# A hybrid decoder layer on one core: three quarters of the output projection moved among the small products of the last head pair

## The chip, the core and the metric

The kernel runs on one of the eight cores of a Trainium2 chip. TensorE (PE) multiplies, and its weight loads are listed apart (PEld); VectorE (DVE), ScalarE (ACT) and GpSimd (POOL) do the elementwise work; SyncE (SP) issues nearly all DMAs. SBUF holds tiles of 128 partitions, and PSUM has eight banks of 128 x 512 float32 values for the results of PE. The metric is the device time of one launch in microseconds, as the median of several runs.

## What is computed

The reference is one decoder layer over 512 tokens and 16 meta tokens, width 1024, in float32:

```
h      = layer_norm([meta, x], ln0)                      # 528 x 1024
proj   = h @ w_in                                        # q, k, v, r/k/v/w/a/g of RWKV-7, two gates
att    = sliding-window attention with sinks (16 heads of 64)
rw     = RWKV-7 time mixing: a recurrence over time, 16 heads of 64
merged = sigmoid(gate_att) * att + sigmoid(gate_rwkv) * rw
h      = layer_norm(ALPHA * h + merged @ w_out, ln1)     # w_out: 1024 x 1024
ff     = square(relu(h @ w_ff1)) @ w_ff2                 # 1024 -> 4096 -> 1024
out    = layer_norm(ALPHA * h + ff, ln2)                 # the 512 tokens
```

The matrix product in the middle, `merged @ w_out`, is the output projection that the change moves.

## The kernel before

**Products.** Each float32 operand of a large product is split into a high and a low part (`split`, L253, two ACT casts of 128 x 512 and two DVE subtractions), and three matmuls stand for one product: high x high, high x low, low x high (`three`, L332; `project_out`, L1390). The normalized input lies in `hhi` and `hlo`, eight tiles k of 128 channels by 528 tokens (L279). A dense unit (`dense`, L348) is one column block of 128 of `w_in` and has eight steps, one for each k.

**Stages.** Heads go in pairs j = 0 to 7, and the loop of L1319 goes through stages s = -1 to 8. In stage s, PE runs the small products of three things: the solve and the state chain of pair s-1 (`solve`, L1277: blocks, start, inverse, fold, seven chain steps, outputs Y, the transposes yt of `rwkv_norm`), the scan preparation of pair s (`scan`, L1262), and attention of pair s-1 (`attend`, L1303: four calls of scores, then turn, out, turn, out, and `merge`, L1193). Between these stand the dense units of the next projections.

**Order.** PE's order is written out by hand: `weave` (L381) goes through a stage's items, each with a due time in microseconds of dense work, and takes dense steps until the due time is reached. Dense time alone counts. The other engines and the DMA queue are ordered by a list scheduler from priorities: what is written first comes first, and `ahead(n)` moves a block n places forward. Each engine executes its own list strictly in order.

**The end of the stages.** In stage 7 the dense units are the two gates of pair 6, the query of pair 7 and the two gates of pair 7. In stage 8 there are none: the solve of pair 7 and the attention of pair 7 (scores due at 2.0, turn at 12.0) run alone. Pairs 0 to 6 leave their merged rows in DRAM (`md`, L1200).

**After the stages.** `merged(j)` (L1368) loads a pair's rows from `md` through one buffer, and writes a high part (ACT) and a low part (DVE) into new tiles `mhi` and `mlo`. Then the PSUM pools of the stages are closed and eight banks opened for the output (four row blocks b of 128 tokens, two column halves n). `project_out` runs k by k for the first four tiles k, and block by block for the last four (`WOL = 4`), so that the rows of block 0 are finished first. Meanwhile `x` is loaded again (`res`), and `norm_rows` (L1359, two DVE operations of 128 x 1024 per block) makes `h` of it. `first_norm` (L1469) adds the accumulators, takes the statistics, normalizes, and transposes back for the feed-forward part: on DVE two additions, two bn_stats, two small operations with a power on POOL between, one normalization, and after eight PE transposes (`tp`) eight ACT operations, two ACT casts and two DVE subtractions. The feed-forward's `up` (L1519) begins with three column blocks on the first 256 tokens (blocks 0 and 1), then on the last 256.

Of the kernel before, what the change touches and what calls it, by code (L numbers as in the profile page):

```python
# [20 lines left out]
P = 128  # L21
D = 1024
# [60 lines left out]
WOL = 4  # L83
# [49 lines left out]
def hybrid_layer_kernel(ctx: ExitStack, tc: tile.TileContext, I: dict, out: bass.AP):  # L133
# [30 lines left out]
    wst = ctx.enter_context(tc.tile_pool(name="wst", bufs=2))  # L164
    p1 = ctx.enter_context(ExitStack())
    hpool = p1.enter_context(tc.tile_pool(name="hpool", bufs=1))
    lz = p1.enter_context(tc.tile_pool(name="lz", bufs=1))
    mg = ctx.enter_context(tc.tile_pool(name="mg", bufs=1, side="right"))
# [798 lines left out]
    def rwkv_norm(j):  # L967
        yn = SS[j]["yn"]
        yt = pch.tile([P, 512], F32, name="yt", tag="ch")
        for b in range(4):  # L970
            pe.transpose(
                yt[:, b * P : (b + 1) * P], yn[:, 2 * b : 2 * b + 2].rearrange("p u i -> p (u i)"),
                ident,
            )
        z = mg.tile([P, SEQ], F32, name="z", tag="z", bufs=ABUF["z"])
        act.activation(z, yt, AF.Identity, bias=vcol("lnx_b", j), scale=vcol("lnx_g", j))
        SS[j]["z"] = z
# [100 lines left out]
    def gate_tile(name, tag, j):  # L1078

        if j == PAIRS - 1:  # L1080
            return ew.tile([P, T], F32, name=name, tag=tag)[:, :SEQ]
        return mg.tile([P, SEQ], F32, name=name, tag=name, bufs=ABUF[name])
# [71 lines left out]
    def attention_turn(j, i):  # L1154
# [3 lines left out]
        for n in range(2):  # L1158
# [6 lines left out]
        act.copy(pall, pv)  # L1165
        dve.tensor_tensor(
            pown, pv, cv("mown").unsqueeze(1).to_broadcast([P, 4, P]), op=ALU.mult
        )
# [24 lines left out]
    def merge(j):  # L1193

        z, bv = SS[j]["z"], aside(mg, SS[j]["bv"], "bvm", ABUF["bv"])
# [3 lines left out]
        if j < PAIRS - 1:  # L1199
            nc.sync.dma_start(md[j], z)  # L1200
        else:
            A["z"] = z
# [49 lines left out]
    gate_att(j - 1)  # L1252
    gate_rwkv(j - 1)
    query(j)
    gate_att(j)
    gate_rwkv(j)
    marks.append(len(units))
# [60 lines left out]
    with tc.manual_schedule(engines={mybir.EngineType.PE}):  # L1318
        for s in range(-1, PAIRS + 1):  # L1319
            if s < PAIRS:  # L1320
# [21 lines left out]
            if 0 < s < PAIRS:  # L1342
                items += attend(s - 1) + join(s - 1, 31.5)
            if s == PAIRS:
                items += attend(s - 1, 2.0, 12.0) + join(s - 1, 31.5)
            weave(items, s < PAIRS)
    pew.close()
    prw.close()

# [13 lines left out]
    p3 = ctx.enter_context(ExitStack())  # L1363
    mT = p3.enter_context(tc.tile_pool(name="mT", bufs=1, side="right"))
    mhi = mT.tile([P, PAIRS, SEQ], F32R, name="mhi")
    mlo = mT.tile([P, PAIRS, SEQ], F32R, name="mlo")

    def merged(j):  # L1368

        m = aside(mT, md[j], "mf", 1) if j < PAIRS - 1 else A["z"]  # L1370
        act.activation(mhi[:, j, :], m, AF.Copy, scale=0.5)
        dve.scalar_tensor_tensor(
            mlo[:, j, :], m, 0.5, mhi[:, j, :].bitcast(F32), op0=ALU.mult, op1=ALU.subtract
        )

    for j in range(PAIRS):
        merged(j)
    ppr.close()
    pa = ctx.enter_context(tc.tile_pool(name="pa", bufs=1, space=PSUM, side="right"))
    p2.close()  # L1380
    p1.close()
    pps.close()
    pb = ctx.enter_context(tc.tile_pool(name="pb", bufs=1, space=PSUM))
    fin = ctx.enter_context(tc.tile_pool(name="fin", bufs=1))
    acc = {
        (b, n): (pa, pb)[b // 2].tile([P, 512], F32, name=f"o{b}{n}", tag=f"acc{(2 * b + n) % 4}")
        for b in range(4) for n in range(2)
    }

    def project_out(k, w, b):  # L1390

        hi, lo = w
        bs = slice(b * P, (b + 1) * P)
        for n in range(2):
            ns = slice(n * 512, (n + 1) * 512)
            first, last = k == 0, k == KT - 1
            pe.matmul(acc[b, n], mhi[:, k, bs], hi[:, ns], start=first, stop=False)
            pe.matmul(acc[b, n], mhi[:, k, bs], lo[:, ns], start=False, stop=False)
            pe.matmul(acc[b, n], mlo[:, k, bs], hi[:, ns], start=False, stop=last)

# [4 lines left out]
    for k in range(KT - WOL):  # L1405
        w = load("w_out", k)
        for b in range(4):
            project_out(k, w, b)
    wo = ctx.enter_context(ExitStack())
    wop = wo.enter_context(tc.tile_pool(name="wo", bufs=1))  # L1410
    wout = []
    for k in range(KT - WOL, KT):
        raw = wst.tile([P, D], F32, name="wraw", tag="wraw", bufs=WB[2])
        nc.sync.dma_start(raw, I["w_out"][k])
        wout.append(
            split(
                raw,
                wop.tile([P, D], F32R, name=f"wohi{k}"),
                wop.tile([P, D], F32R, name=f"wolo{k}"),
            )  # L1420
        )
    for b in range(4):
        norm_rows(res[b], *moments0[b], g0, b0)

    def project(k0, nk, xhi, xlo, n, hold=2, more=None):
# [4 lines left out]
        def add(w, q, b):  # L1430
            hi, lo = w
            bs = slice(b * P, (b + 1) * P)
            for d in range(2):
# [3 lines left out]
                pe.matmul(acc[b], xhi[:, k, bs], hi[:, ws], start=first, stop=False)  # L1437
                pe.matmul(acc[b], xhi[:, k, bs], lo[:, ws], start=False, stop=False)  # L1438
                pe.matmul(acc[b], xlo[:, k, bs], hi[:, ws], start=False, stop=last)  # L1439
# [29 lines left out]
    def first_norm(b, pool_, acc):  # L1469
# [153 lines left out]
```

## Time and profile before

| | us |
|---|---|
| median of 3 runs (lowest, highest) | 1020.75 (1020.67, 1022.77) |
| the profiled execution | 1021.99 |
| its span, first to last instruction | 1020.0 |
| PE busy in the span | 952.6 (93%) |
| DVE busy | 655.7 (64%) |
| ACT busy | 471.7 (46%) |
| POOL busy | 43.8 (4%) |
| mean granted clock of PE | 0.968 |

Times in the trace are counted from the span's start. A busy time is the sum over an engine's instructions with overlaps counted once; matmuls are pipelined, so a matmul's own duration is longer than the distance to the next. A granted clock of 1.00 is full speed. "Idle before" is the engine's empty time ahead of an instruction, with the instruction that ended it.

### The profile page before, as it was taken

To read this page: it belongs to the slowest core of one execution; us is meant where nothing else is said; L and a number is where in the kernel's file an instruction comes from. 1 tells how busy PE (TensorE), PEld (TensorE's weight loads), DVE (VectorE), ACT (ScalarE), POOL (GpSimd) and SP (SyncE) were. 2 spreads that over 40 slices of the span, in tenths; PEclk is the share of its full clock that TensorE was granted. 3 is DMA by queue.
4 is the path that set the end of the run, shared out by engine and by line. 5 is a ranking of instruction groups with operands and counts; after the bars stand their busy time and mean duration, and the time that the engine had idled before them with its cause. 6 is when DMAs were issued, how large, how long until landed. Compare 5 with 4: busy or idle time off the path is not lost.

```text
span 1020.0 us, 19168 instructions
## 1 busy us (share of the span) xinstructions
PE 952.6 (93%) x7533; PEld 801.9 (79%) x7533; DVE 655.7 (64%) x1495; ACT 471.7 (46%) x1238; POOL 43.8 (4%) x108
## 2 busy tenths in 40 slices
PE   4999899999999999999998749999999999999997
PEld 3989688787888878888776637798888888888885
DVE  8678686887887878778784446776542334453336
ACT  6536456574574745846537423463431224343120
POOL 2000000010000100001000000000000000000001
PEclk9999999999999999999999659999999999999999
DMA  7454433224333333332323046013323323323232
GB/s 263 92 145 116 101 79 103 72 68 112 90 97 84 90 104 79 83 101 68 104 72 106 12 159 222 22 62 125 122 85 103 102 81 107 103 88 98 83 104 82
DMA packets 80657, 101.79 MB, mean 100 GB/s; under 512 B 47542, under 2 KB 54440, under 8 KB 80568
## 3 DMA queue, kind: packets, MB, share of 16 engines
q1 hardware_dynamic: 79072, 98.49, 32.7%
q10 hardware_dynamic: 1496, 2.08, 0.6%
q8 instruction: 59, 0.97, 0.4%
q14 instruction: 30, 0.25, 0.1%
HBM read 84.46 MB, written 11.90 MB: 94 GB/s over the span
## 4 chain that ended last, share of the span: by engine, by line
PE 65%; DVE 15%; ACT 12%; DMA 5%; issue 2%; SPq 0%; POOL 0%; DVEq 0%; ACTq 0%; POOLq 0%
PE dps L333 12%; PE dps L334 11%; PE dps L335 10%; PE acc L1437 6%; PE acc L1438 6%; PE acc L1439 6%; ACT Z L746 2%; ACT whi L260 2%; DVE wlo L263 2%; PE av L1180 2%; PE sc L661 2%; DVE AX L886 2%; ACT sb L1151 2%; DVE Xf L770 1%; DVE ftmp L766 1%
## 5 line engine op out<-in xcount | busy, mean ns | idle before, releaser
L263 DVE TENSOR_TENSOR wlo<-wraw,whi 128x512 fp32r<-128x512 f32 x234 | 154.0, 686 | 176.6 <-ACT whi L260 176.0
L260 ACT CAST whi<-wraw 128x512 fp32r<-128x512 f32 x234 | 136.8, 617 | 262.9 <-PE dps L334 132.3
L333 PE MATMUL dps<-hhi,whi 128*128 128x264 f32 (+1 forms) x640 | 219.6, 343 | 1.8 <-ACT whi L260 1.1
L334 PE MATMUL dps<-hlo,whi 128*128 128x264 f32 (+1 forms) x640 | 205.2, 321 | 1.0 <-DVE hlo L314 1.0
L335 PE MATMUL dps<-hhi,wlo 128*128 128x264 f32 (+1 forms) x640 | 204.5, 320 | 0.4 <-DVE wlo L263 0.4
L333 PEld LDWEIGHTS dps<-hhi,whi 128*128 128x128 f32 x640 | 122.5, 191 | 15.2 <-ACT whi L260 1.3
L335 PEld LDWEIGHTS dps<-hhi,wlo 128*128 128x128 f32 x640 | 122.0, 191 | 9.1 <-DVE wlo L263 0.6
L334 PEld LDWEIGHTS dps<-hlo,whi 128*128 128x128 f32 x640 | 122.4, 191 | 6.2 <-DVE hlo L314 1.7
L334 PE MATMUL dps<-h1lo,whi 128*128 128x512 f32 (+1 forms) x264 | 99.4, 377 | 0.0
L335 PE MATMUL dps<-h1hi,wlo 128*128 128x512 f32 (+1 forms) x264 | 99.3, 376 | 0.0
L333 PE MATMUL dps<-h1hi,whi 128*128 128x512 f32 (+1 forms) x264 | 99.2, 376 | 0.0
L1437 PE MATMUL acc<-whi,fhi 128*128 128x512 f32 x240 | 93.4, 389 | 0.0
L1438 PE MATMUL acc<-wlo,fhi 128*128 128x512 f32 x240 | 93.4, 389 | 0.0
L1439 PE MATMUL acc<-whi,flo 128*128 128x512 f32 x240 | 93.4, 389 | 0.0
L334 PEld LDWEIGHTS dps<-h1lo,whi 128*128 128x128 f32 x264 | 49.7, 188 | 9.2 <-DVE h1lo L1493 0.2
L335 PEld LDWEIGHTS dps<-h1hi,wlo 128*128 128x128 f32 x264 | 49.7, 188 | 9.1
L333 PEld LDWEIGHTS dps<-h1hi,whi 128*128 128x128 f32 x264 | 49.6, 188 | 9.1
L1439 PEld LDWEIGHTS acc<-whi,flo 128*128 128x128 f32 x240 | 45.0, 188 | 9.4
L1437 PEld LDWEIGHTS acc<-whi,fhi 128*128 128x128 f32 x240 | 45.0, 188 | 9.4
L1438 PEld LDWEIGHTS acc<-wlo,fhi 128*128 128x128 f32 x240 | 45.0, 188 | 9.3
L899 ACT ACTIVATE Z<-ch,PC 64x64 f32<-64x64 f32 x56 | 17.3, 310 | 39.4 <-DVE Z L897 38.1
L1532 DVE TENSOR_TENSOR rl<-rl 128x512 f32<-128x512 f32 (+1 forms) x35 | 22.6, 645 | 11.8 <-ACT fhi L1531 11.7
(292 smaller groups left out, 1622.2 us busy)
## 6 DMA issues: line engine op xcount, KB each, us to landing
wraw<-in_w_ff_dram SPq DMA_DIRECT2D x64, 512.0 KB, 3.5
wraw<-in_w_in_dram SPq DMA_DIRECT2D x52, 512.0 KB, 4.0
wraw<-in_w_out_dram SPq DMA_DIRECT2D x8, 512.0 KB, 3.9
xt<-in_x_dram SPq DMA_DIRECT2D x4, 512.0 KB, 7.4
Nd<-NT SPq DMA_DIRECT2D x16, 128.0 KB, 2.7
bv<-bv SPq DMA_DIRECT2D x8, 256.0 KB, 2.2
bvm<-bv SPq DMA_DIRECT2D x8, 256.0 KB, 4.0
qs<-qhi SPq DMA_DIRECT2D x16, 128.0 KB, 3.0
```

The source lines that it names most:

```text
L260: act.copy(hi[:n, qs], raw[:n, qs])
L263: dve.tensor_tensor(lo[:n, qs], raw[:n, qs], hi[:n, qs].bitcast(F32), op=ALU.subtract)
L333: pe.matmul(ps, whi, xhi, start=first, stop=False)
L334: pe.matmul(ps, whi, xlo, start=False, stop=False)
L335: pe.matmul(ps, wlo, xhi, start=False, stop=last)
L661: pe.matmul(scs[e][:, c * P : (c + 1) * P], BK[ER[e], 4 * i + c, :], AXg[ER[e], e, 4 * i + c], start=True, stop=True,)
L746: act.copy(Z[2 * i + cc][64 * (1 - e) : 64 * (1 - e) + 64, e, :], vt[64 * cc : 64 * cc + 64, i * P + e * HD : i * P + (e + 1) * HD],)
L886: dve.tensor_tensor(AXg[:, e, cs], AXg[:, e, cs], gqs[e].rearrange("p (c k t) -> p c k t", c=4, k=2), op=ALU.add,)
L1437: pe.matmul(acc[b], xhi[:, k, bs], hi[:, ws], start=first, stop=False)
L1438: pe.matmul(acc[b], xhi[:, k, bs], lo[:, ws], start=False, stop=False)
L1439: pe.matmul(acc[b], xlo[:, k, bs], hi[:, ws], start=False, stop=last)
L1532: dve.tensor_tensor(r, r, r, op=ALU.mult)
```

## The change

The output projection is cut anew. `w_out` is laid out in pairs of k and halves of columns, so that one load of 512 KB holds tiles k = 2q and 2q+1 for one column half n. Tiles k = 0 to 5 of all four row blocks become four dense units of 36 matmuls each (`out_unit`, twelve steps of three matmuls), which stand in stage 8 between the small products of pair 7; k = 6 and 7 stay behind the stages.

- **Rows.** The parts `mhi[k]` and `mlo[k]` are no tiles of their own any more: they are written over `hhi[:, k, 16:]` and `hlo[:, k, 16:]`, which the dense units of stage 7 are the last to read. The feed-forward's first eight rows of `fhi` and `flo` use the same place later.
- **Banks.** The eight accumulators take the banks of the stages one by one: (b 0, 1; n 0) those of the dense units, (b 2, 3; n 0) those of attention, (b 0, 1; n 1) those of the scores and folds, (b 2, 3; n 1) those of the chain `ch` (which also holds yt) and of `Y`.
- **Stage 7.** The merged rows of pairs 0 to 5 are loaded from `md` into six buffers of their own (due at 10.0). The query of pair 7 goes second in place of third. The attention of pair 6 is turned at 20.5 in place of 26.0 and merged at 26.5 in place of 31.5; pairs 6 and 7 keep their merged rows in SBUF. The scores of pair 7 run here (due from 16.5). Three loads of `w_out` are issued at 27.2.
- **Stage 8.** `merged(0)` to `merged(5)` at its start, ahead by 400; turn and out of pair 7 at 1.0 to 5.8; yt at 24.5; merge of pair 7 at 25.5; `merged(7)` at 25.6; the other five loads of `w_out` from within the units.
- **All stages.** The copies out of the turned probabilities (`pall`, `pown`) get `ahead(200)`, and the eviction `z` of yt gets `ahead(600)`. The tiles `z`, `bvm`, `ga` and `gg` move to another pool.
- **Behind the stages.** `res` and its normalization come later: block 3 on POOL (four operations of 128 x 1024), blocks 0 and 1 on DVE just ahead of their part of the projection, block 2 after it. Each block has 12 matmuls left in place of 24. `first_norm` of blocks 0 and 1 goes ahead by 400.

```diff
-WOL = 4
...
-        z = mg.tile([P, SEQ], F32, name="z", tag="z", bufs=ABUF["z"])
-        act.activation(z, yt, AF.Identity, bias=vcol("lnx_b", j), scale=vcol("lnx_g", j))
+        z = at.tile([P, SEQ], F32, name="z", tag="z", bufs=ABUF["z"])
+        with ahead(PRI["chain"]):
+            act.activation(z, yt, AF.Identity, bias=vcol("lnx_b", j), scale=vcol("lnx_g", j))
...
-        act.copy(pall, pv)
-        dve.tensor_tensor(
-            pown, pv, cv("mown").unsqueeze(1).to_broadcast([P, 4, P]), op=ALU.mult
-        )
+        with ahead(PRI["turn"]):
+            act.copy(pall, pv)
+            dve.tensor_tensor(
+                pown, pv, cv("mown").unsqueeze(1).to_broadcast([P, 4, P]), op=ALU.mult
+            )
...
+    mhi = [hhi[:, k, NMETA:] for k in range(KT)]
+    mlo = [hlo[:, k, NMETA:] for k in range(KT)]
+    def merged(j):
+        m = A["m", j]
+        act.activation(mhi[j], m, AF.Copy, scale=0.5)
+        dve.scalar_tensor_tensor(
+            mlo[j], m, 0.5, mhi[j].bitcast(F32), op0=ALU.mult, op1=ALU.subtract
+        )
+    def merged_before():
+        for j, tag in enumerate(("u", "L", "tw", "ta", "Px", "rk")):
+            A["m", j] = ew.tile([P, SEQ], F32, name="mf", tag=tag)
+            nc.sync.dma_start(A["m", j], md[j])
...
+    def project_out(q, n, b, d):
+        hi, lo = wout[q, n]
+        k, bs, ws = 2 * q + d, slice(b * P, (b + 1) * P), slice(d * 512, (d + 1) * 512)
+        first, last = k == 0, k == KT - 1
+        pe.matmul(acc[b, n], mhi[k][:, bs], hi[:, ws], start=first, stop=False)
+        pe.matmul(acc[b, n], mhi[k][:, bs], lo[:, ws], start=False, stop=False)
+        pe.matmul(acc[b, n], mlo[k][:, bs], hi[:, ws], start=False, stop=last)
+    def out_unit(n, blocks, asks):
+        if n == 0 and blocks[0] == 0:
+            with ahead(PRI["dense"]):
+                for j in range(PAIRS - 2):
+                    merged(j)
+        for b in blocks:
+            acc[b, n] = new_bank(b, n, f"o{b}{n}")
+        for q in range(KT // 2 - 1):
+            for d in range(2):
+                for b in blocks:
+                    project_out(q, n, b, d)
+                    yield 3 * 0.227
+            if asks[q]:
+                load_out(*asks[q])
...
+        (0, (0, 1), none),
+        (0, (2, 3), ((0, 1), (1, 1), (2, 1))),
+        (1, (0, 1), none),
+        (1, (2, 3), ((3, 0), (3, 1), None)),
...
+            if s == PAIRS - 1:
+                items += [(10.0, (), merged_before)]
+                items += attend(s - 1, t1=20.5) + join(s - 1, 26.5)
+                items += attend(s, 16.5)[:4]
+                items += [(27.2, (), F(load_out, q, 0)) for q in range(3)]
             if s == PAIRS:
-                items += attend(s - 1, 2.0, 12.0) + join(s - 1, 31.5)
-            weave(items, s < PAIRS)
+                items += attend(s - 1, t1=1.0)[4:] + join(s - 1, 25.5)
+                items += [(2.0, (), F(merged, s - 2)), (25.6, (), F(merged, s - 1))]
+            weave(items, True)
...
+    mean, r = moments0[3]
+    for op, t in zip(
+        (ALU.subtract, ALU.mult, ALU.mult, ALU.add),
+        (mean.to_broadcast([P, D]), g0, r.to_broadcast([P, D]), b0),
+    ):
+        pool.tensor_tensor(res[3], res[3], t, op=op)
...
     for b in range(4):
-        for k in range(KT - WOL, KT):
-            project_out(k, wout[k - KT + WOL], b)
+        if b < 2:
+            norm_rows(res[b], *moments0[b], g0, b0)
+        for n in range(2):
+            for d in range(2):
+                project_out(KT // 2 - 1, n, b, d)
         if 0 < b <= NORMED:
-            first_norm(b - 1, pa, acc)
+            with ahead(400):
+                first_norm(b - 1)
+    norm_rows(res[2], *moments0[2], g0, b0)
+    pps.close()
```

118 lines of the change are left out of this document (44 added, 74 removed).

## The prediction

> **What bounds the kernel now.** I read the page's forty slices first, then busy times of PE by stretch, then the rows of PE's timeline at the ends of the weak stretch.
>
> ```profile
> PE   4999899999999999999998749999999999999997
> PEclk9999999999999999999999659999999999999999
> ```
>
> PE is full nearly everywhere; slices of 25.5 us at 535 to 612 us are the exception, and there the granted clock falls too. The stretches:
>
> ```profile
> 45.00:500.90 455.90, 438.73 (x4567) 375.75 (x4565) 361.12 (x960) 260.77 (x777) 25.87 (x66) 0.99 0.35 94
> 500.90:552.20 51.30, 51.05 (x529) 39.67 (x527) 34.15 (x99) 29.20 (x92) 2.96 (x3) 1.00 0.27 66
> 552.20:608.20 56.00, 31.19 (x410) 25.26 (x409) 26.33 (x55) 20.04 (x60) 1.63 (x1) 0.61 0.26 90
> 608.20:661.90 53.70, 50.86 (x216) 40.90 (x217) 36.73 (x54) 18.91 (x40) 1.66 (x3) 0.93 0.40 135
> 661.90:1020.00 358.10, 350.55 (x1619) 292.92 (x1617) 165.74 (x258) 113.64 (x212) 4.62 (x5) 0.99 0.29 96
> ```
>
> Columns: length, busy PE, PEld, DVE, ACT, POOL, granted clock, DMA share, GB/s. Stage 7 (second row) has PE busy 51.05 of 51.3 us at clock 1.00. The third row is the end of pair 6 and all of stage 8, without dense work: PE is busy 31.19 of 56.0 us at clock 0.61. The fourth is the output projection. What stands at the borders:
>
> ```profile
> 551.92 0.40 PE L335 MATMUL gp<-sghi,gwl 128*128 128x512 f32 x1
> 598.69 1.12 PE L971 MATMUL yt<-con,gyn 128*128 128x128 f32 x4 [4.12 <-DVE gyn L964]
> 608.19 0.77 PE L1397 MATMUL o<-whi,mhi 128*128 128x512 f32 x1 [8.38 <-ACT mhi L1371]
> 661.92 0.36 PE L333 MATMUL dps<-h1hi,whi 128*128 128x256 f32 x1
> ```
>
> The last gate's product ends at 552.2, the last small product (yt) at 599.8, then PE waits 8.38 us for rows to merge and be read back; `up` starts at 661.92. So in 552.2 to 661.9, **109.7 us**, PE waits for latencies, and does it at half speed. Whatever PE work is ready there is nearly free: that is the room the change wants to use.
>
> **The change part by part.** First PE's own work in that room at full clock.
>
> ```profile
> 613.13 0.39 PE L1397 MATMUL o<-whi,mhi 128*128 128x512 f32 x1
> ...
> 632.17 0.39 PE L1397 MATMUL o<-wohi,mhi 128*128 128x512 f32 x1
> ```
> ```profile
> 648.38 1.03 PE L1484 MATMUL tp<-con,res 128*128 128x128 f32 x8
> 649.17 0.49 PE L1397 MATMUL o<-wohi,mhi 128*128 128x512 f32 x1
> ```
>
> 84 matmuls lie between the first two rows: 0.2267 us each, so the projection's 192 need 43.5 us wherever they stand. Three groups of transposes `tp` before `up` need 0.8 us each, 2.4. The small products, among them pair 6's late attention and pair 7's scores, which the change moves into stage 7, come to 31.19 x 0.61 = 19.0 us at full clock. Sum 64.9 us. Packed without any wait, the change would gain 109.7 - 64.9 = **44.8 us**. That contains the idle time, the half clock, and the read-back of `md`: six of its loads move forward on SP's queue into stage 7, where the DMA share is 0.27, ahead of pair 7's own loads (due at 16.0); the seventh and the store of pair 6 fall away. I cost these loads at nothing; a late one costs its 3.3 us once. The merged rows overwrite `hhi` tile by tile behind the last gate's steps, 0.7 us apart, so the first unit finds k = 0 early. What takes back part of it:
>
> *S1, ACT's list around the border of stages 7 and 8.*
>
> ```profile
> 541.20:552.20 11.00, 11.00 (x57) 8.89 (x55) 3.38 (x7) 10.75 (x36) 1.63 (x1) 1.00 0.16 31
> ```
> ```profile
> 539.68 1.09 PE L722 MATMUL tr<-con,BK 128*128 128x128 f32 x8
> ```
> ```profile
> 543.25 2.15 ACT L1151 ACTIVATE sb<-sb,sm 128x128 f32<-128x128 f32 x7
> ```
> ```profile
> L1145 ACT ACTIVATE sb<-sb,nm 128x128 f32<-128x128 f32 x8 | 3.1, 388 | 0.0
> ...
> L1151 ACT ACTIVATE sb<-sb,sm 128x128 f32<-128x128 f32 x8 | 2.6, 390 | 0.6 <-DVE sm L1149 0.5
> ...
> L1371 ACT ACTIVATE mhi<-mf 128x512 fp32r<-128x512 f32 x1 | 0.6, 629 | 3.4 <-DMA mf<-md 3.4
> ```
>
> ACT is busy 10.75 of the last 11 us of stage 7. There the change adds pair 7's softmax (3.1 + 2.6 plus accumulator reads, some 7 us), one more split and six casts `mhi` of 0.63 us, and asks for pair 6's turn at 20.5, that is some 2.5 us after `tr` (due 19.0, at 539.68), at 542.2, while the probabilities it needs are scaled from 543.25 to 544.5. That is 2 us of PE waiting, with every dense step and scan product of the stage queued behind; the backlog may add as much again at pair 7's turn, due 1.0 into stage 8, though the wait also gives ACT time. The casts are wanted only every 1.4 us. I take 3 us, between 0.5 and 7 (the whole softmax in the way).
>
> *S2, waits within stage 8.* The second column half's units for blocks 2 and 3 begin in the bank of yt, directly behind it, and so wait for its eviction:
>
> ```profile
> 599.85 0.78 ACT L976 ACTIVATE z<-yt,vc 128x512 f32<-128x512 f32 x1 [4.64 <-PE yt L971]
> ```
>
> 1.2 us with the way there; the units of these blocks, and all dense work, are queued behind. Otherwise stage 8 resembles the earlier stages, in which PE idled 455.90 - 438.73 = 17.2 us in some seven: 2.5 each, 0.25 in stage 7; I take 1.5. Together 2.7, between 1.2 and 6.
>
> *S3, the end of the projection.* Here the cover is gone. Before, each block's last 24 matmuls gave DVE 5.4 us to normalize the block before; now 12 give 2.7.
>
> ```profile
> L1473 DVE SCALAR_TENSOR_TENSOR res<-res,o 128x512 f32<-128x512 f32 x8 | 5.5, 688 | 4.1 <-PE o L1399 4.0
> ...
> L1361 DVE SCALAR_TENSOR_TENSOR res<-res,rs,rvln_b 128x1024 f32<-128x1024 f32 x4 | 5.0, 1280 | 0.7 <-DMA rvln_b<-in_rows_dram 0.7
> ...
> L1454 DVE BATCH_NORM_STATS2 fst<-res 128x6 f32<-128x512 f32 x6 | 3.8, 683 | 0.0
> L1493 DVE TENSOR_TENSOR h1lo<-h1f,h1hi 128x512 fp32r<-128x512 f32 x4 | 2.8, 689 | 0.3 <-ACT h1hi L1492 0.2
> ...
> L1478 DVE TENSOR_SCALAR res<-res,fmv,rsf 128x1024 f32<-128x1024 f32 x3 | 2.4, 813 | 2.1 <-POOL rsf L228 2.1
> ```
> ```profile
> 649.01 1.86 ACT L1487 ACTIVATE h1f<-tp,vc 128x128 f32<-128x128 f32 x5 [9.71 <-PE tp L1484]
> ...
> 652.47 0.62 ACT L1492 CAST h1hi<-h1f 128x512 fp32r<-128x512 f32 x1
> ```
>
> One block costs DVE 2 x 0.69 + 2 x 0.68 + 0.4 for the small ones + 0.7 waiting for POOL + 0.81 = 4.6 us up to its transposes; ACT then takes 4.1 (649.01 to 653.09). Count from the start of the last 48 matmuls: block 0 is accumulated at 2.7, normalized at 7.3, block 1 at 11.9, its rows back at 11.9 + 0.9 + 4.1 + 0.7 = 17.6. PE is done at 10.9 + 1.6 = 12.5, and `up` needs blocks 0 and 1: 5.1 us of waiting, 3.1 if it may start on the first four k. I take 4.0. Blocks 2 and 3 follow on DVE: four subtractions 2.8, the norm of `res` 2 x 1.28, two blocks 9.2 bring 26.5, and block 3's rows 32.2; the first halves of `up` keep PE to some 26. A second wait, 0 to 5.9: I take 3.0. Both let the clock fall:
>
> ```profile
> 639.36 0.50 PE L1397 MATMUL o<-wohi,mhi 128*128 128x512 f32 x1 [2.34 <-ACT mhi L1371]
> ```
> ```profile
> 637.00:643.50 6.50, 4.16 (x12) 3.26 (x12) 2.35 (x4) 1.67 (x3) 0.00 (x0) 0.74 0.29 95
> ```
>
> After 2.34 us without work, 4.16 busy us ran at 0.74: 1.1 us lost, twice 2.2. And `res`:
>
> ```profile
> 599.89 1.28 SPq L1403 DMA_DIRECT2D res<-in_x_dram  x3
> ```
> ```profile
> 610.06 2.48 DVE L1360 SCALAR_TENSOR_TENSOR res<-res,mv,rvln_g 128x1024 f32<-128x1024 f32 x2 [1.25 <-DMA rvln_g<-in_rows_dram]
> ```
>
> Its loads left SP right after yt, whose input frees the pool, and the row vector arrived 11.4 us after yt began. The new end starts 10.3 us after yt (2.1 and twelve steps of 0.68), block 0 is ready at 13.0, its norm of `res` at 11.4 + 2.56 = 14.0: 1.0 late, 3.6 with block 1's in front. S3 is 4.0 + 3.0 + 2.2 + 1.0 = 10.2, between 4.2 and 16.7.
>
> Block 3's four POOL operations lie outside the trace; the nearest rows are POOL's copy and DVE's 1.28:
>
> ```profile
> L709 POOL COPY AX<-con 64x512 f32<-64x512 f32 x16 | 10.2, 636 | 172.8 <-PE axt L701 172.4
> ```
>
> 1.3 us each at least, 5 in all, and POOL is empty (1.66 of 53.7 us): nothing, unless the power of a `first_norm` queues behind one. The Trainium skill, GPSIMD Engine Reference, section Engine selection, calls two-input work about twice as slow there as on VectorE; by that each is an estimated 2.5 us, one queued power makes S3 larger by as much, and the gain falls by 2.5.
>
> *G, earlier stages.* `pall` and `pown` move ahead everywhere:
>
> ```profile
> PE av L1180 <- DVE pown L1166: 3.8, 5, 0.8
> PE av L1180 <- ACT pall L1165: 3.8, 5, 0.8
> ```
>
> PE lost 7.6 us to them up to 551. Something else is pushed back on ACT, so I take 2.0, between -2 and 6.
>
> **Sum:** 44.8 - 3.0 - 2.7 - 10.2 + 2.0 = **30.9 us** less. The profiled execution took 1021.99 (span 1020.0), so 991.1; the median of the runs lies 1.24 lower: **990 us**.
>
> **Rivals.**
>
> *A, all covered.* List order absorbs ACT's backlog, `up` starts on the first k: S1 0.5, S2 1.2, S3 4.2: 40.9 less, 980. For it: stage 7 runs the same mixture without idle time. Against: DVE's 4.6 us per block.
>
> *C, waits at their upper ends:* S1 7, S2 6, S3 16.7, G 0: 15.1 less, 1006. For it: ACT at 10.75 of 11, and strict lists.
>
> *D, slower: the clock stays at half in stage 8.* Its dense units stand between steps that wait; if the gate sees too little work, all of it runs as here:
>
> ```profile
> 609.60 0.63 PE L1397 MATMUL o<-whi,mhi 128*128 128x512 f32 x1
> ...
> 610.88 0.63 PE L1397 MATMUL o<-whi,mhi 128*128 128x512 f32 x1
> ```
>
> 0.427 us per matmul. 144 matmuls cost 28.8 us more, the stage's small products (some 15 us) about 9.5: 38.3. Then 44.8 - 38.3 - 15.9 + 2.0 = -7.4: 1028. It decides from 81% of the stage at half clock (30.9/38.3). Against: 1.00 in stage 7. The Trainium skill, TensorE: Matmul & The Clock Gate, section A second HAM failure mode: psum-queue depth-cycling, says that small gaps between groups while banks are cycled let the clock swing; the row at 639.36 shows it after one gap, stage 7 does not show it for a mixture.
>
> *E, the units don't get between:* if their rows, weights or banks are late, PE waits at the first dense step and the small products run alone as before. Left are the waits for `mf` (8.38 + 2.34 + 0.5) with their slow clock, 3.7, less some 5 of S3: 10 less, 1011.
>
> **How the numbers follow.** Forecast 0.46 (its own range 984 to 996), A 0.17, C 0.26, E 0.06, D 0.05. The range takes in A and C with their edges, 977 to 1007. About 0.2% can be told from no change: faster 0.94, same 0.01, slower 0.05.
>
> **What would show it.** Stage 8 as one stretch of some 50 us, PE over 90% busy, clock near 1.00 (D: 0.5; E: idle time first, then dense work in one piece). Waits of `pt` for `sb` near 20.5 and 1.0 tell S1, of the first matmul behind yt for `z` S2, of the first `up` for `h1hi` S3. `up` should start near 631 (661.92 - 30.9). Wrong I would be by a DVE list that holds the merge of pair 7 behind `res`, which I can't see from here.

## The result, and the profile after

The changed kernel took **1009.73 us** as the median of seven runs (1006.05 to 1015.08); the kernel before, 1020.75 in the same comparison. The ratio is 0.9891, with a 95% interval of 0.9862 to 0.9920: 11 us less, where 31 were forecast. The profiled execution took 1007.33, its span 1005.4, at a mean clock of 0.985. One execution of the experiments below, the profiled one of e1, took 1289.94 us at a mean clock of 0.669; neither its time nor its trace is used.

PE and its clock in forty slices, here of 25.1 us:

```profile
PE   4999899999999999999999998699999999999996
PEclk9999999999999999999999999799999999999999
```

The hole of before at 535 to 612 us has closed. A smaller one stands at 628 to 653 us: one slice with PE at 6 tenths and the clock at 7. The stretches, with the columns of before (length, busy PE, PEld, DVE, ACT, POOL, granted clock, DMA share, GB/s):

```profile
499.37:552.00 52.63, 50.69 (x545) 39.41 (x545) 38.70 (x111) 27.73 (x90) 2.85 (x3) 1.00 0.32 82
552.00:613.00 61.00, 58.03 (x538) 42.89 (x536) 29.86 (x54) 26.96 (x74) 2.20 (x2) 0.97 0.27 94
613.00:624.40 11.40, 11.40 (x50) 8.98 (x48) 10.83 (x4) 2.29 (x4) 10.63 (x4) 1.00 0.31 128
624.40:639.72 15.32, 4.05 (x18) 3.15 (x17) 14.64 (x26) 7.94 (x21) 1.50 (x2) 0.67 0.30 96
639.72:1005.40 365.68, 355.43 (x1624) 295.43 (x1624) 170.98 (x268) 115.20 (x214) 5.04 (x6) 0.99 0.29 97
```

The rows are stage 7, stage 8 up to the last quarter of the projection, that quarter, the end up to `up`, and the rest. Stage 8 works as it was meant to: PE is busy 58.03 of 61.0 us at clock 0.97 (before, 31.19 of 56.0 at 0.61), and 144 of the 192 matmuls are done in it. The last quarter itself has no gap. Then come 15.32 us in which PE is busy for 4.05, with the clock at 0.67. PE's instructions with a wait ahead of them, in brackets:

```profile
561.93 0.91 PE L1160 MATMUL pt<-con,sb 128*128 128x128 f32 x3 [1.46 <-ACT sb L1150]
563.33 0.33 PE L1160 MATMUL pt<-con,sb 128*128 128x128 f32 x1 [0.48 <-ACT sb L1150]
...
604.76 0.50 PE L1244 MATMUL o<-whi,hhi 128*128 128x512 f32 x1 [0.93 <-ACT z L975]
```
```profile
630.25 1.97 PE L1512 MATMUL tp<-con,res 128*128 128x128 f32 x8 [5.74 <-DVE res L1506]
634.05 1.97 PE L1512 MATMUL tp<-con,res 128*128 128x128 f32 x8 [1.83 <-DVE res L1506]
639.72 0.58 PE L331 MATMUL dps<-h1hi,whi 128*128 128x256 f32 x1 [3.70 <-ACT h1f L1515]
...
650.74 1.09 PE L1512 MATMUL tp<-con,res 128*128 128x128 f32 x8 [0.37 <-DVE res L1506]
...
654.52 0.51 PE L331 MATMUL dps<-h1hi,whi 128*128 128x256 f32 x2 [1.98 <-ACT h1hi L1520]
```

First the two waits of S1 and the one of S2; then 5.74 + 1.83 + 3.70 us ahead of `up`, which starts at 639.72, and two more behind it. The long wait is for `res`, so the next view is DVE's list in these microseconds:

```profile
613.57 5.20 DVE L1438 SCALAR_TENSOR_TENSOR res<-res,mv,rvln_g 128x1024 f32<-128x1024 f32 x2 [0.99 <-DMA rvln_g<-in_rows_dram]
618.70 6.25 DVE L1439 SCALAR_TENSOR_TENSOR res<-res,rs,rvln_b 128x1024 f32<-128x1024 f32 x2
624.87 1.27 DVE L1501 SCALAR_TENSOR_TENSOR res<-res,o 128x512 f32<-128x512 f32 x2
```

These are blocks 0 and 1: two operations, each on both blocks, and the first addition of an accumulator. In the kernel before one such operation took 1.28 us, so two pairs would be 5.1; here they take 5.20 + 6.25 = 11.45. At the same time POOL normalizes block 3:

```profile
612.43 1.91 POOL L1451 TENSOR_TENSOR res<-res,mv 128x1024 f32<-128x1024 f32 x1 [11.41 <-DMA res<-in_x_dram]
614.42 3.27 POOL L1451 TENSOR_TENSOR res<-res,rvln_g 128x1024 f32<-128x1024 f32 x1
617.77 2.76 POOL L1451 TENSOR_TENSOR res<-res,rs 128x1024 f32<-128x1024 f32 x1
620.60 3.26 POOL L1451 TENSOR_TENSOR res<-res,rvln_b 128x1024 f32<-128x1024 f32 x1
```

11.2 us in all. The two lists interlock: each POOL operation but the first is long by about one DVE operation, and DVE's last one ends at 624.95, 1.1 us behind POOL's last (620.60 + 3.26 = 623.86). The first matmul of the last quarter starts at 613.20, so block 0's accumulators were complete at about 613.2 + 12 x 0.232 = 616.0, and the first addition starts at 624.87.

### The profile page after: what moved, and what is told of

It is laid out like the page before. It is cut to its first block, busy times and chain, and to the rows that moved or that the text cites. A ratio compares the mean times of both kernels' runs of the same rounds, so it can differ in the third digit from the quotient of the medians.

```text
span 1005.4 us, 19165 instructions
## 1 busy us (share of the span) xinstructions
PE 948.8 (94%) x7533; PEld 792.4 (79%) x7533; DVE 657.7 (65%) x1493; ACT 469.9 (47%) x1238; POOL 55.2 (5%) x112
## 4 chain that ended last, share of the span: by engine, by line
PE 67%; DVE 17%; ACT 9%; issue 3%; DMA 2%; SPq 0%; POOL 0%; DVEq 0%; ACTq 0%; POOLq 0%
PE dps L331 12%; PE dps L332 11%; PE dps L333 11%; PE acc L1465 6%; PE acc L1467 6%; PE acc L1466 6%; ACT Z L744 2%; DVE wlo L261 2%; PE sc L659 2%; PE av L1180 2%; DVE ftmp L764 1%; DVE AX L884 1%; DVE Xf L768 1%; PE o L1244 1%; ACT whi L258 1%
## 5 line engine op out<-in xcount | busy, mean ns | idle before, releaser
L258 ACT CAST whi<-wraw 128x512 fp32r<-128x512 f32 x242 | 141.8, 618 | 281.8 <-PE dps L332 135.5
L261 DVE TENSOR_TENSOR wlo<-wraw,whi 128x512 fp32r<-128x512 f32 x242 | 159.6, 685 | 172.0 <-ACT whi L258 171.5
L331 PEld LDWEIGHTS dps<-hhi,whi 128*128 128x128 f32 x640 | 122.3, 191 | 15.3 <-issue 1.4
L1465 PE MATMUL acc<-whi,hhi 128*128 128x512 f32 x128 | 50.7, 396 | 0.0
L1467 PE MATMUL acc<-whi,hlo 128*128 128x512 f32 x128 | 50.4, 394 | 0.0
L1466 PE MATMUL acc<-wlo,hhi 128*128 128x512 f32 x128 | 50.0, 391 | 0.0
L1465 PE MATMUL acc<-whi,fhi 128*128 128x512 f32 x112 | 43.6, 389 | 0.0
L1466 PE MATMUL acc<-wlo,fhi 128*128 128x512 f32 x112 | 43.6, 389 | 0.0
L1467 PE MATMUL acc<-whi,flo 128*128 128x512 f32 x112 | 43.6, 389 | 0.0
L744 ACT COPY Z<-vt 64x64 f32<-64x64 f32 x128 | 26.5, 207 | 9.0 <-PE vt L737 7.6
```

Of the source, the lines that this page charges most:

```text
L258: act.copy(hi[:n, qs], raw[:n, qs])
L261: dve.tensor_tensor(lo[:n, qs], raw[:n, qs], hi[:n, qs].bitcast(F32), op=ALU.subtract)
L331: pe.matmul(ps, whi, xhi, start=first, stop=False)
L744: act.copy(Z[2 * i + cc][64 * (1 - e) : 64 * (1 - e) + 64, e, :], vt[64 * cc : 64 * cc + 64, i * P + e * HD : i * P + (e + 1) * HD],)
L1465: pe.matmul(acc[b], xhi[k][:, bs], hi[:, ws], start=first, stop=False)
L1466: pe.matmul(acc[b], xhi[k][:, bs], lo[:, ws], start=False, stop=False)
```

## Experiments

Two distances within a profiled execution are compared beside the times, since the first 160 us differ by up to 8.5 us from one execution to the next (the first yt starts between 159.5 and 168.0), also in kernels that are alike there: from the start of yt's last transpose to the start of `up`, and from there to the end of the span.

| kernel | median us | ratio to before, 95% interval | yt to `up` | `up` to end |
|---|---|---|---|---|
| before | 1020.75 | 1 | 62.5 | 358.1 |
| changed | 1009.73 | 0.9891 (0.9862 to 0.9920) | 36.1 | 365.7 |
| changed, again (e9) | 1010.68 | 0.9913 (0.9892 to 0.9934) | 36.2 | 365.6 |
| no POOL (e1) | 1007.50 | 0.9874 (0.9847 to 0.9900) | | |
| no POOL, again (e10) | 1006.32 | 0.9869 (0.9851 to 0.9888) | 29.9 | 370.5 |
| loads reordered (e11) | 1006.30 | 0.9882 (0.9854 to 0.9910) | 35.0 | 364.3 |
| reordered, no POOL (e5) | 1006.09 | 0.9877 (0.9850 to 0.9904) | 31.4 | 367.2 |
| rows not normalized (e2) | 998.66 | 0.9775 (0.9748 to 0.9802) | 26.7 | 363.6 |
| turns later (e6) | 1009.05 | 0.9912 (0.9893 to 0.9931) | 36.2 | 367.9 |
| `hhi` shifted (e3) | 1007.32 | 0.9870 (0.9845 to 0.9894) | 36.2 | 367.8 |
| before, lists ahead (e4) | 1017.87 | 0.9968 (0.9950 to 0.9986) | 58.4 | 358.1 |
| early rows (e7) | 998.04 | 0.9805 (0.9783 to 0.9827) | 26.6 | 362.9 |
| early rows, turns later (e8) | 996.98 | 0.9790 (0.9771 to 0.9810) | 26.5 | 363.9 |
| the same, end reordered (e12) | 986.89 | 0.9696 (0.9674 to 0.9718) | 23.8 | 360.3 |

The theory is that the late and slow normalization of the input rows takes back most of what is missing. Its rivals: the chain of additions, statistics and evictions behind it would be just as late without it; the waits in stage 8 (S1, S2), or slower matmuls, take it.

**e1 and e10: block 3 on DVE.**

```diff
-    mean, r = moments0[3]
-    for op, t in zip(
...
-        pool.tensor_tensor(res[3], res[3], t, op=op)
...
+    norm_rows(res[3], *moments0[3], g0, b0)      # behind that of block 2
```

> Block 3's rows of the input are normalized on DVE, behind block 2's, and no longer on POOL; nothing else changes. Theory contention (POOL's four operations and DVE's four run at the same time and hold each other up): DVE's four operations ahead of block 0's addition take 1.28 us each in place of 2.6 to 3.1, 5.1 us in place of 11.5; the first transposes of the last projection come near 624 in place of 630.25, the feed-forward starts near 633 in place of 639.7, and the launch is 4 to 6 us shorter than the changed kernel (1004 to 1006), as block 3 now costs DVE 2.6 us. Rival late rows (the input's rows and the row vectors arrive too late, whatever POOL does): the DVE operations keep 2.6 to 3.1 us, the transposes stay within 1 us of 630, the time within 1 us of the changed kernel's 1009.7.

> The kernel with block 3 normalized on DVE once more, for the times of its operations at an undisturbed clock. Theory 1 (POOL's four operations slow DVE's): DVE's eight normalizing operations take 1.28 us each, the first two blocks are done by 613.6 + 5.1 = 618.7 in place of 624.9, and up starts 2 to 4 us earlier, though block 3's 2.6 us now stand on DVE. Theory 2 (it is the late input rows alone that cost, and POOL's share hides behind them): the operations are shorter, but up starts within 1 us of 639.7, and the time is within 1 us of the changed kernel's.

The trace of this kernel is that of e10. DVE's list for blocks 0 and 1, and then two of PE's waits:

```profile
614.95 2.48 DVE L1438 SCALAR_TENSOR_TENSOR res<-res,mv,rvln_g 128x1024 f32<-128x1024 f32 x2 [1.22 <-DMA rvln_g<-in_rows_dram]
617.35 2.48 DVE L1439 SCALAR_TENSOR_TENSOR res<-res,rs,rvln_b 128x1024 f32<-128x1024 f32 x2
```
```profile
634.64 0.58 PE L331 MATMUL dps<-h1hi,whi 128*128 128x256 f32 x1 [3.69 <-ACT h1f L1508]
...
649.86 1.97 PE L1505 MATMUL tp<-con,res 128*128 128x128 f32 x8 [3.40 <-DVE res L1499]
```

Each pair takes 2.48 us: it was POOL that had doubled them. `up` starts 6.3 us earlier behind yt (29.9 for 36.2). But now block 3's 2.6 us stand on DVE ahead of the statistics of blocks 2 and 3; their transposes wait 3.40 us at 649.86, and 4.9 us are given back behind `up`. So POOL's four operations were far from free, and moving them to DVE at that place is no cure: 2.2 (e1) and 4.4 us (e10) by the medians, beside the run of the changed kernel nearest to each, and 1.4 by the two distances. `up` came as much earlier as e1's expectation had it, and more than e10's; but e1 itself gave 2.2 us of the launch where 4 to 6 were expected, since block 3 costs 4.9 us behind `up` where the expectation counted its 2.6 of work.

**e11 and e5: the order of six loads,** with POOL as in the change (e11) and without (e5).

```diff
+    g0 = rowvec("ln0_g")
+    nc.sync.dma_start(res[0], I["x"][0:P, :])
+    b0 = rowvec("ln0_b")
-    for b in range(4):
+    for b in range(1, 4):
         nc.sync.dma_start(res[b], I["x"][b * P : (b + 1) * P, :])
-    g0, b0 = rowvec("ln0_g"), rowvec("ln0_b")
```

> The changed kernel with the order of six loads changed alone: row ln0_g, input rows of block 0, row ln0_b, then the other blocks; POOL still normalizes block 3. With the kernel that also takes POOL away at 1006.1, this one tells how much of that is the order. If lateness and POOL's contention each cost their own time: 1 to 2.5 us less than the changed kernel. If the order alone does it: 3 to 4 us less. If POOL eats up what the earlier rows give (its operations then lie beside DVE's just as before): within 1 us of the changed kernel.

> The changed kernel with two edits: the row ln0_g is loaded first, then the input rows of block 0, then ln0_b and the other blocks, and block 3 is normalized on DVE instead of POOL. Theory 1 (the end of the projection is set by the input rows, which reach DVE at about 613 us and are then worked on at less than half of DVE's speed because POOL works at the same time): DVE starts its first normalization 3 to 4 us earlier and each operation takes 1.28 us, so the first group of turns on TensorE comes near 623 to 625 in place of 630.25, up starts near 634 to 636 in place of 639.72, and the time falls by 4 to 6 us against the changed kernel, to 1004 to 1006. Theory 2 (the end is set by what follows on DVE and ACT, whatever the rows do, since leaving the normalization out altogether still let up start only at 630.81): up starts within 2 us of 639.72 and the time is 1008 to 1010.

Block 0 is normalized from 610.8 on in e11, before POOL starts at 616.1. Yet `up` comes only 1 us earlier. DVE and POOL of e11 show why:

```profile
616.88 1.28 DVE L1503 SCALAR_TENSOR_TENSOR res<-res,o 128x512 f32<-128x512 f32 x2
618.07 1.28 DVE L1484 BATCH_NORM_STATS2 fst<-res 128x6 f32<-128x512 f32 x2
619.27 3.02 DVE L1439 SCALAR_TENSOR_TENSOR res<-res,rs,rvln_b 128x1024 f32<-128x1024 f32 x1
...
622.33 2.26 DVE L261 TENSOR_TENSOR wlo<-wraw,whi 128x512 fp32r<-128x512 f32 x1
624.51 0.14 DVE L225 TENSOR_SCALAR rsf<-fmv 128x1 f32<-128x1 f32 x1
627.34 0.81 DVE L1508 TENSOR_SCALAR res<-res,fmv,rsf 128x1024 f32<-128x1024 f32 x1 [2.09 <-POOL rsf L226]
```
```profile
624.12 2.67 POOL L1453 TENSOR_TENSOR res<-res,rvln_b 128x1024 f32<-128x1024 f32 x1
```

The additions and the bn_stats keep their 0.64 us apiece beside POOL; the two-tensor operations `res x r + b` (L1439, 3.02 for 1.28) and `wlo` (2.26 for 0.69) do not. And the small value `rsf`, ready at 624.65, needs POOL for a power, which stands behind block 3's last operation: DVE waits 2.09 us. By the medians the order brings 4.4 us beside e9, by the two distances 2.5 (1.2 ahead of `up`, 1.3 behind); that is about as much as taking POOL away, and both together bring no more (1006.1). Which case of e11's expectation holds stays open: the distances fit the first, the medians the second. Theory 1 of e5, `up` at 634 to 636 for 639.72, is met when counted from yt (31.4 for 36.1), but the order brings nothing on top of leaving POOL out: in e10, without the order, it is 29.9. In e5 the first transposes come 18.8 us behind yt (627.03), in e10 20.8; but DVE then takes normalizing operations of blocks 2 and 3 (1.26 us at 629.29, 1.23 at 631.19) before it has finished block 1, whose transposes wait 4.56 us.

**e2: without the normalization of the input rows.** The three `norm_rows` ahead of `first_norm` and the POOL loop go.

> Leaves out the normalization of the input's rows (on DVE and POOL); the raw rows are added to the projection. Theory cover (each block's 4.6 us of DVE work in the first norm stands against 2.7 us of matmuls, as the prediction had it): PE still waits 3 to 5 us ahead of the feed-forward, which starts near 629. Rival (the normalization alone is behind all the waits at the end of the projection, by contention and by late rows): the waits there fall below 1.5 us in all, the feed-forward starts near 626. Against the changed kernel either gives 10 to 14 us, 996 to 1000.

```profile
630.80 0.38 PE L331 MATMUL dps<-h1hi,whi 128*128 128x256 f32 x1 [3.08 <-ACT h1f L1508]
```

Of the 7.6 us for `res` 0.4 are left, but 3.08 us ahead of `up` remain, for ACT's evictions. 26.7 us from yt to `up` is what the chain behind the accumulators takes by itself; the normalization cost 9.4 us on top, and about 2 behind `up`. Of the two expectations it is the first, cover, that holds: 3.5 us of waits where the rival had less than 1.5. 998.7 is far from 990 still.

**e7: the rows 40 us earlier.** Pair 7's gates go to other buffers, so the place of the pairs' working rows is free in stage 8.

```diff
+    def early_rows():            # behind merged(0) to merged(5)
+        pew.close()
+        pool_ = pxe.enter_context(tc.tile_pool(name="xe", bufs=1))
+        for name in ("ln0_g", "ln0_b"):
...
+            nc.sync.dma_start(t, row.to_broadcast([P, D]))
+            xe.append(t)
+        for b in range(4):
+            t = pool_.tile([P, D], F32, name=f"xe{b}")
+            nc.sync.dma_start(t, I["x"][b * P : (b + 1) * P, :])
+            xe.append(t)
+    def early_norm(b):           # due at 8, 12, 16, 20 of stage 8
+        (mean, r), t = moments0[b], xe[2 + b]
+        dve.scalar_tensor_tensor(t, t, mean, xe[0], op0=ALU.subtract, op1=ALU.mult)
+        dve.scalar_tensor_tensor(t, t, r, xe[1], op0=ALU.mult, op1=ALU.add)
...
+    for b in range(4):
+        nc.sync.dma_start(res[b], xe[2 + b])     # behind yt
```

> The changed kernel with the input rows fetched some 40 us earlier: the last pair's two gates lie in other buffers, so that the space of the pairs' working rows is free in stage 8, takes the two rows and the four input blocks there, and DVE normalizes all four blocks in place beside the dense matmuls; POOL normalizes none. When yt has been read the results are copied by DMA to where the residual is kept. Theory 1 (all that the normalization costs at the end is its late start): the time comes to that of the kernel that leaves the normalization out, 998.7, within 2.5 us, with up starting near 631. Theory 2 (DVE is the bound in stage 8: 33 of its 48 us are busy between 552 and 600, and 10.2 us more delay the last pair's chain): up starts at 634 to 638 and the time is 1002 to 1006.

The eight operations, and the one wait that is left ahead of `up`:

```profile
L1241 DVE SCALAR_TENSOR_TENSOR xe<-xe,mv,xeln_g x4: 1270/1275/1285, 575.1 to 585.6; 128x1024 f32<-128x1024 f32 x4
L1242 DVE SCALAR_TENSOR_TENSOR xe<-xe,rs,xeln_b x4: 1267/1273/1285, 576.5 to 586.9; 128x1024 f32<-128x1024 f32 x4
```
```profile
637.12 0.38 PE L331 MATMUL dps<-h1hi,whi 128*128 128x256 f32 x1 [3.82 <-ACT h1f L1529]
```

All eight take 1.27 us, between 575 and 588, and stage 8 is no longer for it (first yt to last 442.5 us; the changed kernel 443.6). With the normalization it has the time of e2, which is without it: 998.0 and 998.7, 26.6 and 26.7 us from yt to `up`. (`up` at 637.12 looks like theory 2, but this execution had its first yt at 168.0, 8 us later than the changed kernel's.) That settles the theory: at this place the normalization costs nothing, at the other one 9.5 us ahead of `up` and about 12 in all.

**e6 and e8: the turns 2 us later** (`attend(s - 1, t1=3.0)[4:]` in place of 1.0); e8 has it on top of e7, and the last unit takes block 3 before block 2, as yt lies in block 2's bank.

> The changed kernel with one number changed: the two turns of the last pair's scores stand 2 us later in stage 8 (at 3.0 in place of 1.0 of its plan), behind dense matmuls. Theory (step S1: TensorE runs dry at the border of the stages because ACT has not scaled the scores yet, 1.46 + 0.48 us of waiting and some 3 us at half clock behind them): the wait of pt for sb in stage 8 goes, the clock stays at 1.00 through 560 to 570, and the time falls by 2.5 to 3.5 us against the changed kernel, to 1006 to 1007.5. Rival (a wait taken away in a stretch that dense work fills only shifts the work; the last pair's chain of small products sets the end of the stage, not the sum of TensorE's work): the wait goes but the first product of the last quarter comes as late as before, and the time stays within 1 us of 1009.7.

> The kernel with the early input rows, with the turns of the last pair's scores 2 us later in the plan and the last unit's two blocks in the other order, so that the bank from which z is still being read is taken last. If the waits are worth their length and the half clock behind them: 2.5 to 4 us less than with the early rows alone, 994 to 997, which lies in the range of the forecast. If they are only shifted: within 1 us of the kernel with the early rows alone.

562 to 570 us in the changed kernel, then in e6:

```profile
562.00:566.00 4.00, 3.52 (x77) 2.33 (x78) 2.29 (x4) 3.95 (x13) 0.00 (x0) 0.83 0.62 204
566.00:570.00 4.00, 4.00 (x58) 2.84 (x56) 1.22 (x4) 1.83 (x7) 0.00 (x0) 0.74 0.14 58
```
```profile
562.00:566.00 4.00, 4.00 (x82) 3.00 (x82) 3.38 (x8) 3.98 (x14) 0.00 (x0) 1.00 0.18 45
566.00:570.00 4.00, 2.96 (x46) 2.21 (x45) 1.77 (x5) 3.82 (x13) 0.00 (x0) 1.00 0.66 227
```

The turns no longer wait and the clock stays at 1.00, but other steps of the chain now wait for ACT (0.23 and 0.80 us), and the time is that of the changed kernel: the rival holds for e6. In e8 the wait for z fell from 0.93 to 0.23 us as well; 996.98 lies at the edge of both expectations, and 1 us less than e7 can't be told from nothing.

**e3: 16 more columns ahead of `hhi` and `hlo`** (the rows that serve as stationary operand then start at a multiple of 128 bytes; `vdif` gives up one of two buffers for the space).

> The changed kernel with the tokens' rows of the input tile starting at a multiple of 128 bytes (a row of 544 columns, tokens from column 32, in place of 528 and 16), and one small attention tile with one buffer in place of two to make room. Theory alignment: matmuls whose stationary operand lies in these rows take 389 ns in place of 397 and follow each other in 0.2267 us in place of 0.232; 384 in the feed-forward and 192 in the projection, 3 to 4 us off the launch, more if the stages' dense units gain too. Rival (the distance of rows or the tile's place doesn't matter, the 8 ns come from the traffic beside them): 397 ns stays, the time within 1 us of the changed kernel.

The feed-forward's first matmul with `hhi` and with `fhi` as stationary operand in the changed kernel, durations as lowest, median, highest in ns; then with `hhi` in e3:

```profile
L1465 PE MATMUL acc<-whi,hhi x128: 392/397/398, 734.5 to 975.1; 128*128 128x512 f32 x128
...
L1465 PE MATMUL acc<-whi,fhi x112: 389/389/393, 756.7 to 996.9; 128*128 128x512 f32 x112
```
```profile
L1465 PE MATMUL acc<-whi,hhi x128: 389/395/404, 738.1 to 978.8; 128*128 128x512 f32 x128
```

The 8 ns stay nearly as they were: neither this start nor this distance of the rows removes them, and the reason is open. The median is 2.4 us below the changed kernel's, but the two distances (36.2 and 367.8) show no gain, so none is claimed.

**e4: the kernel before with `pall`, `pown` and z ahead** as in the change, and nothing else.

> The kernel before with one part of the change: the copies of the turned probabilities go ahead by 200 and the eviction of the transposed state output by 600. Theory G (this part is what starts stage 7 at 499.4 in place of 501.0): stage 7 starts 1.6 us earlier, and the launch is 1 to 3 us shorter than before, 1018 to 1020. Rival (stage 7's earlier start comes from the tiles' other pool or the query's order): no difference from before within 0.5 us.

3.3 us less by the ratio (1.4 to 5.1). From the first yt to stage 7 it takes 339.3 us for 340.2, the changed kernel 339.4: 0.8 to 0.9 us of G. The rest of what its trace shows lies between yt and `up`, 58.4 us for 62.5: PE's three waits for merged rows are 7.62, 0.29 and 1.27 us for 8.38, 0.50 and 2.34, and behind the last of them the clock is 1.00 from 640 to 650 for 0.83. Why these rows come earlier isn't shown; the changed kernel no longer reads them back there, so this part of the gain is not in it.

**e9: the changed kernel once more,** as a measure beside e10 to e12.

> The changed kernel itself, unedited, so that the three kernels beside it are compared on one chip. 1007 to 1011 by either theory.

1010.68; the distances in the table agree to 0.1 us.

**e12: another order at the end.** It starts from e8. The first weight of the last quarter is loaded ahead of time, into the place of `g2` and `b2`, and the merge of pair 7 goes ahead by 500.

```diff
+    for n in range(2):
+        for b in range(2):
+            for d in range(2):
+                project_out(KT // 2 - 1, n, b, d)
+    for b in range(2, 4):
+        with ahead(400):
+            first_norm(b - 2)
+        for q, n in ((3, 0), (2, 1), (3, 1)):    # (2, 1) was in the last dense unit
+            for d in range(2):
+                project_out(q, n, b, d)
```

> The kernel with the early input rows, the later turns and the other order of the last unit, 997.0, with the end of the projection in another order: the last quarter of blocks 0 and 1 comes first, and the third quarter of blocks 2 and 3 in the second half of the columns, which was the end of the dense units, comes behind it, beside the norm of blocks 0 and 1. The number of matmuls is the same. If what is still exposed is the chain of DVE and ACT behind the last product of block 1 (up waits 3.9 us for ACT's h1f): that product comes 2.7 us earlier, up starts 2 to 3 us earlier, and the time is 993.5 to 995.5. If ACT's and DVE's own work in that stretch is the bound and not its start (16 evictions and four copies of ACT lie between 622 and 630): within 1 us of 997.0, or more if the last pair's merge is delayed by the earlier split of a weight.

The first addition in e8 and in e12 (yt began 3.1 us earlier in e12); PE ahead of `up` in e8, then in e12; and the first 15.8 us of `up` in the same order:

```profile
613.99 0.69 DVE L1515 SCALAR_TENSOR_TENSOR res<-res,o 128x512 f32<-128x512 f32 x1 [2.20 <-PE o L1268]
```
```profile
608.10 0.69 DVE L1531 SCALAR_TENSOR_TENSOR res<-res,o 128x512 f32<-128x512 f32 x1 [1.56 <-PE o L1280]
```
```profile
629.94 0.58 PE L331 MATMUL dps<-h1hi,whi 128*128 128x256 f32 x1 [3.91 <-ACT h1f L1529]
```
```profile
623.28 1.09 PE L1542 MATMUL tp<-con,res 128*128 128x128 f32 x8 [0.76 <-DVE res L1536]
624.25 0.38 PE L331 MATMUL dps<-h1hi,whi 128*128 128x256 f32 x1
```
```profile
629.90:645.70 15.80, 15.73 (x106) 15.52 (x107) 10.01 (x20) 11.79 (x30) 1.10 (x2) 0.80 0.21 67
```
```profile
624.20:640.00 15.80, 15.75 (x130) 15.40 (x129) 11.61 (x23) 14.47 (x36) 0.55 (x1) 1.00 0.30 99
```

Behind yt, the first addition comes 2.8 us earlier and `up` 2.7. The wait of 3.91 us is gone, `up` follows its transposes without one, and the clock is 1.00 where it was 0.80 for 15.8 us. Behind `up` it is 3.6 us less; 130 matmuls for 106 in these 15.8 us, 24 more at some 0.12 us each, are 2.9 of them. The expectation had the first part and not the second. Of the 9.3 us between the two profiled executions the other 3.0 lie ahead of yt, and there ahead of the first yt (159.5 for 162.7), where executions of like kernels differ by more; they are not put down to the edit. The ratios differ by 9.6 us, with an interval of some 2 us on each, so that a part of the gain may lie where the two distances don't see it. At 986.9 this is the fastest version, 22 us (by the ratios) to 24 us (by the medians) below the changed kernel run beside it.

## Why the prediction was wrong

Its packing held, its price for the end did not. Its terms put the start of the last quarter at 552.2 - 2.0 + 5.7 + 19.0 + 32.6 = 607.5, `up` 18.6 later (10.9 + 1.6 + 4.0 + 1.0 + 1.1) at 626.1, and the end 363.0 behind that (358.1, a transpose group 0.8, the second wait 3.0, its clock 1.1). The "631" of its last part took all 30.9 us off ahead of `up` and so contradicts its own terms. The whole range, 977 to 1007, missed 1009.73. Against the trace, 16.3 us of span are to be found:

| | forecast | measured | more |
|---|---|---|---|
| G, start of stage 7 | -2.0 | -1.6 | 0.4 |
| small products at full clock | 19.0 | 22.6 | 3.6 |
| 144 matmuls in stage 8 | 32.6 | 33.4 | 0.8 |
| S1 and S2, waits and clock | 5.7 | 6.0 | 0.3 |
| start of the last quarter to `up` | 18.6 | 26.7 | 8.1 |
| `up` to end | 363.0 | 365.7 | 2.7 |

The rows come to 15.9; the other 0.4 us are short gaps of PE in stages 7 and 8.

- **S3, the step that failed.** Two sentences did it: that the input rows would make block 0 "1.0 late", and that block 3's four POOL operations cost nothing because POOL is empty. The addition came 624.87 - 616.0 = 8.9 us after the accumulators. Begun at 613.57, both blocks' norms would have ended at 618.7 undisturbed: 2.7 us late, within the prediction's bound of 3.6. The other 6.2 are the doubling by POOL, for which it had nothing. e10 shows them gone ahead of `up` (29.9 for 36.1), e7 the whole term: 9.5 us where the prediction had 1.0. The prediction asked whether POOL had time, and not what DVE reads while POOL reads. Its waits for the chain itself were right in kind: 3.7 us ahead of `up` for ACT's `h1f` (4.0 forecast), 0.37 + 1.98 + 0.2 behind it (3.0).
- **The small products** were mis-sized. 31.19 x 0.61 scales a busy time by the clock; in the mixture the same products take 50.69 + 58.03 - 51.05 (stage 7's work of before) - 33.4 (144 x 0.232) - 1.7 (58.03 x 0.03, the clock of 0.97) = 22.6. Part of it shows in the first matmul of each dense step, the one behind a small product:

```profile
L1244 PE MATMUL o<-whi,hhi 128*128 128x512 f32 x48 | 21.3, 443 | 0.9 <-ACT z L975 0.9
L1245 PE MATMUL o<-wlo,hhi 128*128 128x512 f32 x48 | 19.4, 404 | 0.0
```

48 x (443 - 404) ns = 1.9 us, an estimate from these durations. The other 1.7 of the 3.6 isn't located.

- **The projection's matmuls** stand mostly 0.232 us apart, not 0.2267 (621.79 to 624.11 us, ten of them), now that their stationary rows lie in `hhi` and `hlo`: 0.8 us in stage 8. So do the feed-forward's with these rows, and 384 x 5.3 ns = 2.0 us would be most of the last row; e3 tried to show it by taking the difference away and could not.
- **S1, S2, G** held in the sum, in part by luck. At pair 7's turn `pt` waited for `sb` as S1 had it, 1.46 + 0.48 us, and z cost 0.93 where S2 took 2.7 in all. At pair 6's turn in stage 7 `pt` did not wait; what waited there were the scores of pair 7, for DVE:

```profile
535.77 0.39 PE L1122 MATMUL sp<-khi,qs 128*128 128x256 f32 x1 [0.39 <-DVE gg L1109]
545.18 0.36 PE L1122 MATMUL sp<-khi,qs 128*128 128x256 f32 x1 [1.03 <-DVE sb L1125]
```

The 1.7 of clock had no term in S1 or S2. Of G's 1.6 us 0.8 are counted from the first yt (339.4 for 340.2); the other 0.8 lie ahead of it, where executions differ.

- **Rivals.** D and E are refuted by stage 8 (clock 0.97, units between the small products); that E's 1011 is the number nearest to the result is chance. C, 1006, had the right kind, but its 3.6 for `res` was too low, and the small products were in none of the cases. And what the prediction feared, pair 7's merge behind `res` on DVE, did not happen: the merge was over at 608.3, `res` began at 613.57.

## What to carry to other kernels

When work moves off the end of a stage, the chain that it covered becomes the end: count it from the last product that the next consumer needs, and put that product first (e12: the same matmuls in another order, 6 us from yt to the end). An idle engine is not a free one: ask which operands its work shares with the busy engine, and which small operation of the chain stands in its queue (e11). And where something is wanted late but its inputs are there early, as with these rows, look for a place to do it 40 us sooner before looking for another engine.

## What the runs showed of the hardware

- **POOL against DVE.** Operations of DVE with two tensors in SBUF took 1.85 to 3.4 us beside POOL's tensor_tensor in place of 1.28; additions out of PSUM and bn_stats in between did not change (0.64 us). POOL's own took 1.91 us when it started alone (1.5 times DVE's 1.28; the prediction's estimate was 2.5) and up to 3.27 otherwise, and each of DVE's four operations on blocks 0 and 1 ended some 1.1 us behind one of POOL's. The Trainium skill, SBUF — State Buffer, section Who interferes with whom, says that a DVE instruction with two SBUF inputs contends with a GpSimd instruction that reads SBUF, and calls the ports that the two share an exclusive lock, for which the order of issue decides who blocks; the rows above agree, in both directions.
- **The clock after short waits.** It was 0.83 and 0.74 in the two 4 us behind waits of 1.46 and 0.48 us, and 0.67 over the 15.3 us ahead of `up` with waits of 5.74, 1.83 and 3.70; behind the 0.93 us at 604, and behind e4's 1.27 us at 639.78, it stayed at 1.00. In e8 a wait of 3.91 us ahead of `up` left 0.80 for the 15.8 us after it.
- **Stationary rows in `hhi`:** 397 ns for 389 in the feed-forward, unexplained. It isn't the place of these rows alone: the third matmul of a gate's product, `gp<-sghi,gwl`, which doesn't read `hhi`, took 397 too in the kernel before (eight of eight), and ten of the projection's matmuls with rows in `hhi` and `hlo` stood 0.228 us apart (608.12 to 610.40).
